# One group of half-row products per half of the heads, in four PSUM banks, in place of two groups in two

## The chip, the cores and the metric

The kernel runs on one core of a Trainium2 chip. The metric is the device time of one execution in microseconds (us). The kernel before takes 2233.55 us, the median of three runs (2233.27 to 2233.9).

An engine is named here as in the profile: PE is TensorE (matmuls; PEld are its weight loads), DVE is VectorE, ACT is ScalarE, POOL is GpSimd, SP is SyncE, whose queue issues most of the DMAs.

## The reference

One decoder layer on 256 tokens of width 2048, in float32: a SwiGLU feed-forward block, a token mixer, a cross-attention into 256 memory rows, a second feed-forward block and a last RMSNorm. The change lies in the mixer's RWKV-7 branch, 16 heads of 64:

```
r, k, v, xw, xa, xg = split(token_shift(p, mu))
w_log = -softplus(-(w0 + tanh(xw) @ w2)) - 0.5          # decay
a     = sigmoid(a0 + xa @ a2)                           # rate
kk    = k * k_k / norm(k * k_k)
k     = k * (1 + (a - 1) * k_a)
y     = scan over t:  S = S * decay_t + (S @ -kk_t) (kk_t * a_t)^T + v_t k_t^T ;  y_t = S @ r_t
```

Here `xw` and `xa` have 64 columns each, so the products with `w2` and `a2` contract over 64 rows. The scan is worked out in two chunks of 128 tokens. In a chunk each head has a triangular system, whose 128x128 matrix holds the products of the removal keys of any two tokens, cut to its lower triangle. These products too contract over 64 rows, the size of a head.

## The kernel before

**The stream of weights.** All large products take 128 tokens by 512 columns and run over the weights in pieces of two times 128 rows. Each float32 weight is divided into a high part (a cast on ACT, line 365) and a low part (a subtraction on DVE, line 366), and each product is three matmuls (lines 442 to 444). SP's queue loads the weights in the order of a plan (line 316). Two pieces ahead of the one in use are divided already.

**The side work.** All else in the mixer is written as generators in groups (`feat`, `attn`, `ew`, `chain`, `norm` and others). In `product`, after each six matmuls of the weight stream, `bg.tick()` lets every group go on by one step, to its next `yield`. `idle(n)` is n steps of nothing. The group `ew` runs one generator at a time, in this order: `decay_and_rate`, `removal_keys` for the first and the second half of the heads, `substitute`, and later `receptances` and `values`. What is traced in this order gives each instruction its priority; the scheduler that draws up the engines' programs takes of the ready ones the one of highest priority. So an instruction whose bank isn't empty can be passed by a later one.

**The banks.** PSUM has eight banks here: three with the tag `acc` (the sums of the weight products), three with the tag `mm` and two with the tag `tr`. `mm()` and `tr()` take the next free bank of their tag. Transposes (`feat`, line 630), the attention's second product (line 996, emptied by lines 1003 and 1004) and the head sums of the keys (line 1158) use `tr`.

**Decay and rate.** `decay_and_rate` waits until attention has been traced, loads `w2` into partitions 0 to 63 and `a2` into 64 to 127 (lines 1059 and 1060), and then goes over the two halves of the heads (`h`) and over two pairs of 128-column pieces in each (`q`). A group is four calls (line 1073): two pieces, and for each the decay (rows 0 to 63, first bank) and the rate (rows 64 to 127, second bank). Four sigmoids on ACT (line 1080) empty the two banks, and two steps of idling follow. Afterwards come the running sums over time on DVE (line 1087).

**Triangular systems.** `removal_keys(h)` makes the keys of eight heads and ends with two groups, one per chunk (`c`): eight calls (line 1195), four pairs of heads, the even ones on rows 0 to 63 into one bank and the odd ones on rows 64 to 127 into another. A step later DVE masks both banks into the tile `lt` (line 1201), POOL issues the DMA of `lt` to the DRAM tile `ld` (line 1206), and a step ends. Before that, POOL multiplies the keys (lines 1185 and 1186). `substitute` then loads the diagonal blocks back through SP's queue (line 1216), solves them row by row on DVE (lines 1223 and 1228) and writes the result to `xd` (line 1230), which the chains of `pairs` (first product at line 1326) use after `values`.

Of the kernel before, what the change touches and what calls it, by code (L numbers as in the profile page):

```python
# [9 lines left out]
AF = mybir.ActivationFunctionType  # L10
# [5 lines left out]
P = 128  # L16
T = 256
# [119 lines left out]
def decoder_layer(ctx: ExitStack, tc: tile.TileContext, a: dict, out: bass.AP):  # L137
    nc = tc.nc
    act, dve, pool, pe = nc.scalar, nc.vector, nc.gpsimd, nc.tensor
# [23 lines left out]
    def mm():  # L163
        return ps.tile([P, 512], F32, tag="mm", name="mm")

    def tr():
        return ps.tile([P, 512], F32, tag="tr", name="tr", bufs=2)

    def wait_for(name):
        while name not in bg.seen:  # L170
            yield

    def idle(n):
        for _ in range(n):
            yield
# [68 lines left out]
    w0, a0, k_k, k_a, r_k, ln_w, ln_b = (cols[:, 80 + i * 8 : 88 + i * 8] for i in range(7))  # L244
# [25 lines left out]
    for entry in weight_plan(a):  # L270
# [10 lines left out]
        for k in range(k0, k0 + nk, 2 * KU):  # L281
            u = len(units)
            units += [(v, k + i, c, 512) for v, c in zip(w, c0) for i in (0, KU)]
            for i in range(2):
                q = (k - k0) // KU + i
# [587 lines left out]
    with tc.tile_pool(name="mx", bufs=1, reuse_waits="tile") as sp:  # L873
# [3 lines left out]
        def t4(name, shape=(P, 4, T), dt=F32):  # L877
            return sp.tile(list(shape), dt, tag="t4", name=name, bufs=N4)
# [165 lines left out]
        def halves(x):  # L1044
            return x[:].rearrange("p c (b t) -> p (c b) t", b=2)

        xwa = sp.tile([P, T], F32, name="xwa")
# [4 lines left out]
        cs, ee, e0, aa, at_, bt, dec = [], [], [], [], [], [], []  # L1052
        keep2 = keep[:].rearrange("p c t -> p (c t)")

        def decay_and_rate():
            yield from wait_for("small")
            yield from wait_for("attn")
            wa = t4("wa", (P, RW))
            pool.dma_start(wa[0:64, :], W["rwkv_w2"])
            pool.dma_start(wa[64:128, :], W["rwkv_a2"])  # L1060
            with tc.issue_after(at["exp"].ins):
                act.activation(xwa[0:64, :], xwa[0:64, :], AF.Tanh)
                act.activation(xg[:], xg[:], AF.Sigmoid)
            yield
            for h in range(2):
                cs.append(t4("cs"))
                aa.append(t4("aa"))
                for q in (0, 2):
                    b = [mm() for _ in range(2)]
                    for i in range(2):  # L1070
                        for e in range(2):
                            r, c = slice(64 * e, 64 * e + 64), (4 * h + q + i) * P
                            pe.matmul(
                                b[e][:, i * T : (i + 1) * T], wa[r, c : c + P], xwa[r, :],
                                start=True, stop=True,
                            )
                    for i in range(2):
                        for e, (dst, bias) in enumerate(((cs[h], w0), (aa[h], a0))):
                            c = 4 * h + q + i
                            sigmoid = act.activation(  # L1080
                                dst[:, q + i, :], b[e][:, i * T : (i + 1) * T], AF.Sigmoid,
                                bias=bias[:, c : c + 1],
                            )
                    yield from idle(2)
            for h in range(2):
                for c in range(4):
                    dve.tensor_tensor_scan(
                        cs[h][:, c, :], keep2, cs[h][:, c, :], 0.0, ALU.mult, ALU.add
                    )
                    if c % 2:  # L1090
                        yield
                c3 = halves(cs[h])
                mid = stat.tile([P, 8], F32, tag="mid", name="mid")
                dve.tensor_copy(mid[:], c3[:, :, 63])
                dve.tensor_tensor(
                    c3, c3, mid[:].unsqueeze(2).to_broadcast([P, 8, P]), ALU.subtract
                )
                dec.append(stat.tile([P, 4], F32, tag="dec", name="dec"))
                dve.tensor_tensor(dec[h][:], cs[h][:, :, 127], mid[:, 1:8:2], ALU.add)
                yield  # L1100
                with tc.issue_after(sigmoid.ins):
                    act.activation(dec[h][:], dec[h][:], AF.Exp, scale=-DECAY)

                ee.append(t4("ee", (P, 8, P)))
                e0.append(stat.tile([P, 8], F32, tag="e0", name="e0"))
                with tc.issue_after(sigmoid.ins):
                    act.activation(e0[h][:], mid[:], AF.Exp, scale=DECAY)
                    act.activation(ee[h][:], c3, AF.Exp, scale=-DECAY)
                yield
                act.activation(cs[h][:], cs[h][:], AF.Exp, scale=DECAY)  # L1110
                yield
            bg.seen.add("decay")

        bg.spawn("ew", decay_and_rate())


# [27 lines left out]
        def removal_keys(h):  # L1144
            yield from wait_for(f"k{h}")
            yield from wait_for("decay")
            ei = cs[h]
            kk, sq = t4("kk"), t4("sq")
            for i in range(4):
                c = 4 * h + i  # L1150
                act.activation(kk[:, i, :], kt[h][:, i, :], AF.Copy, scale=nk_k[:, c : c + 1])
            yield
            act.activation(sq[:], kk[:], AF.Square)
            yield
            for i in (0, 2):
                b = tr()
                sq2 = sq[:, i : i + 2, :].rearrange("p c t -> p (c t)")
                pe.matmul(b[:], bdones[:], sq2, start=True, stop=True)
                act.activation(sq2, b[:], AF.Sqrt)
                yield  # L1160
                dve.tensor_scalar(sq2, sq2, 1e-12, None, ALU.max)
                for k in range(2):
                    dve.reciprocal(sq[:, i + k, :], sq[:, i + k, :])
                    yield from idle(2)
            dve.tensor_tensor(kk[:], kk[:], sq[:], ALU.mult)
            yield
            at_.append(t4("at"))
            for later, before in ((slice(1, P), ee[h][:, :, : P - 1]), (0, e0[h][:])):
                dve.scalar_tensor_tensor(
                    halves(at_[h])[:, :, later], halves(kk)[:, :, later], DOWN, before,  # L1170
                    ALU.mult, ALU.mult,
                )
            yield
            dve.scalar_tensor_tensor(kk[:], kk[:], -1.0, aa[h][:], ALU.mult, ALU.mult)
            yield
            dve.tensor_tensor(kk[:], kk[:], ei[:], ALU.mult)
            bt.append(kk)
            yield
            for i in range(4):
                c = 4 * h + i  # L1180
                dve.tensor_scalar(
                    aa[h][:, i, :], aa[h][:, i, :], k_a[:, c : c + 1], ok_a[:, c : c + 1],
                    ALU.mult, ALU.add,
                )
            pool.tensor_tensor(kt[h][:], kt[h][:], aa[h][:], ALU.mult)
            pool.tensor_tensor(aa[h][:], kt[h][:], ei[:], ALU.mult)

            for c in range(2):
                cs_ = slice(c * P, (c + 1) * P)
                lt = t4("lt", (P, 8, P))  # L1190
                b = [mm() for _ in range(2)]
                for j in range(4):
                    for e in range(2):
                        r = slice(64 * e, 64 * e + 64)
                        pe.matmul(
                            b[e][:, j * P : (j + 1) * P], at_[h][r, j, cs_], bt[h][r, j, cs_],
                            start=True, stop=True,
                        )
                yield
                for e in range(2):  # L1200
                    dve.tensor_tensor(
                        lt[:, 4 * e : 4 * e + 4, :], b[e][:].rearrange("p (j s) -> p j s", j=4),
                        mask_l[:].unsqueeze(1).to_broadcast([P, 4, P]), ALU.mult,
                    )
                o = h * 16 + c * 8
                pool.dma_start(ld[:, o : o + 8, :], lt[:])
                yield
            yield
# [25 lines left out]
        for h in range(2):  # L1234
            kt.append(t4("kt"))
            columns4(kt[h], 8 + 4 * h, f"k{h}")
            bg.spawn("ew", removal_keys(h))
# [321 lines left out]
        for n in range(4):  # L1559
            s = t4("x2", (P, 2, 512))  # L1560
# [62 lines left out]
        for h in (0, 2):  # L1623
            b = tr()
# [17 lines left out]
    with tc.tile_pool(name="f2", bufs=1, reuse_waits="tile") as sp:  # L1642
# [51 lines left out]
        for t in range(2):  # L1694
            m, r = (stat.tile([P, 1], F32, tag=e, name=e) for e in ("ms", "rs"))
# [58 lines left out]
```

## Time and profile before

| what | value |
| --- | --- |
| median of three runs | 2233.55 us |
| profiled execution | 2234.97 us, its span 2233.2 us |
| granted TensorE clock | 0.999 |
| products for decay and rate (line 1073) | 32 instructions, 846.6 to 860.4 us |
| products for the triangular systems (line 1195) | 64 instructions, 905.6 to 944.1 us |
| masks of the systems (line 1201) | 8 instructions, 0.68 us each |
| substitution (lines 1223 to 1230) | 970.5 to 1027.5 us |

The page of the profile gives busy times, the chain of work that ended last and the costliest groups. The timeline view lists instructions in order of time: start, length, engine, line, operation, output and inputs, shapes, count, and in brackets the idle time before them with what ended it. Neighbours of the same kind stand in one row. The length of a matmul is longer than the time from its start to the next one's, since matmuls overlap; so the text goes by starts.

### The profile page before, as it was taken

Reading aid. Unit: us, or ns where it says so; the run is one execution under the profiler, and the core shown is the slowest. Engines: PE = TensorE matmul, PEld = TensorE weight load, DVE = VectorE, ACT = ScalarE, POOL = GpSimd, SP = SyncE. Lnnn points to the kernel's source line nnn. Section 1 sums busy time; section 2 is a strip of 40 time slices with the busy share of each in tenths; the row PEclk is TensorE's granted clock in tenths of the full one; section 3 lists DMA queues with packets and bytes.
Section 4 is the critical chain, followed back from the end, with each engine's and each line's share of the span. In section 5 each row is a group of like instructions: output and inputs, shape, how many; then the busy total and the mean of one; then the engine's idle time right before and its main releaser. Section 6 shows DMA issues by size and latency. Waiting matters only on the chain.

```text
span 2233.2 us, 28140 instructions
## 1 busy us (share of the span) xinstructions
PE 2218.3 (99%) x10520; PEld 1825.6 (82%) x10520; DVE 1828.1 (82%) x2366; ACT 1248.2 (56%) x1626; POOL 116.6 (5%) x181
## 2 busy tenths in 40 slices
PE   9999999999999999999999999999999999999998
PEld 7888888888888877788888888888888888888876
DVE  7999989898989477877657656547999999999997
ACT  7555555555556468544444546556665565655654
POOL 0000000000001001200221030001000000000000
PEclk9999999999999999999999999999999999999999
DMA  8565566556556545677768688658575576556563
GB/s 303 193 211 199 189 208 201 194 189 212 202 189 199 173 134 153 188 236 208 225 202 277 200 262 282 188 160 279 195 251 194 193 245 207 203 208 220 198 240 137
DMA packets 231561, 466.02 MB, mean 209 GB/s; under 512 B 15521, under 2 KB 17921, under 8 KB 231425
## 3 DMA queue, kind: packets, MB, share of 16 engines
q1 hardware_dynamic: 222256, 438.08, 59.3%
q0 software_dynamic: 7648, 23.52, 3.4%
q10 hardware_dynamic: 1520, 2.63, 0.3%
q8 instruction: 82, 1.34, 0.3%
q14 instruction: 55, 0.44, 0.1%
HBM read 440.49 MB, written 23.59 MB: 208 GB/s over the span
## 4 chain that ended last, share of the span: by engine, by line
PE 91%; DVE 4%; DMA 3%; issue 1%; ACT 1%; SPq 0%; POOL 0%; POOLq 0%; ACTq 0%; DVEq 0%
PE acc L442 18%; PE acc L443 18%; PE acc L444 18%; PE mm L442 8%; PE mm L443 8%; PE mm L444 8%; PE tr L443 2%; PE tr L630 2%; PE tr L442 2%; PE tr L444 2%; DVE lo L366 2%; PE mm L1390 1%; DMA raw<-in_ffn_w_up_dram 1%; PE tr L1326 1%; PE mm L949 0%
## 5 line engine op out<-in xcount | busy, mean ns | idle before, releaser
L365 ACT CAST hi<-raw 128x1024 fp32r<-128x1024 f32 (+1 forms) x768 | 754.9, 993 | 685.6 <-PE acc L444 500.9
L366 DVE TENSOR_TENSOR lo<-raw,hi 128x1024 fp32r<-128x1024 f32 (+1 forms) x768 | 882.5, 1152 | 298.7 <-ACT hi L365 296.2
L442 PE MATMUL acc<-hi,xhi 128*128 128x512 f32 (+1 forms) x1134 | 446.9, 395 | 2.3 <-ACT hi L365 0.8
L443 PE MATMUL acc<-lo,xhi 128*128 128x512 f32 (+1 forms) x1134 | 440.5, 389 | 0.8 <-DVE lo L366 0.8
L444 PE MATMUL acc<-hi,xlo 128*128 128x512 f32 (+1 forms) x1134 | 440.2, 388 | 0.0
L442 PEld LDWEIGHTS acc<-hi,xhi 128*128 128x128 f32 x1134 | 212.8, 188 | 49.4 <-issue 3.7
L443 PEld LDWEIGHTS acc<-lo,xhi 128*128 128x128 f32 x1134 | 213.1, 188 | 44.9 <-DVE lo L366 2.1
L444 PEld LDWEIGHTS acc<-hi,xlo 128*128 128x128 f32 x1134 | 213.0, 188 | 44.2 <-issue 1.3
L373 ACT CAST thi<-raw 128x1024 fp32r<-128x1024 f32 x192 | 200.3, 1052 | 75.2 <-DVE raw L396 50.6
L374 DVE TENSOR_TENSOR tlo<-raw,thi 128x1024 fp32r<-128x1024 f32 x192 | 232.1, 1217 | 0.8 <-ACT thi L373 0.2
L442 PE MATMUL mm<-hi,xhi 128*128 128x512 f32 x402 | 156.6, 389 | 0.0
L443 PE MATMUL mm<-lo,xhi 128*128 128x512 f32 x402 | 156.5, 389 | 0.0
L444 PE MATMUL mm<-hi,xlo 128*128 128x512 f32 x402 | 156.4, 389 | 0.0
L444 PE MATMUL acc<-hi,hlo 128*128 128x512 f32 x372 | 145.4, 391 | 0.0
L443 PE MATMUL acc<-lo,hhi 128*128 128x512 f32 x372 | 145.3, 391 | 0.0
L442 PE MATMUL acc<-hi,hhi 128*128 128x512 f32 x372 | 145.0, 390 | 0.0
L442 PEld LDWEIGHTS mm<-hi,xhi 128*128 128x128 f32 x402 | 75.5, 188 | 16.3 <-ACT hi L365 0.5
L443 PEld LDWEIGHTS mm<-lo,xhi 128*128 128x128 f32 x402 | 75.5, 188 | 15.8
L444 PEld LDWEIGHTS mm<-hi,xlo 128*128 128x128 f32 x402 | 75.5, 188 | 15.7
L443 PEld LDWEIGHTS acc<-lo,hhi 128*128 128x128 f32 x372 | 69.8, 188 | 14.4
L444 PEld LDWEIGHTS acc<-hi,hlo 128*128 128x128 f32 x372 | 69.9, 188 | 14.1
L442 PEld LDWEIGHTS acc<-hi,hhi 128*128 128x128 f32 x372 | 69.9, 188 | 14.1
(400 smaller groups left out, 3548.7 us busy)
## 6 DMA issues: line engine op xcount, KB each, us to landing
raw<-in_ffn_w_down_dram SPq DMA_DIRECT2D x88, 1024.0 KB, 5.2
raw<-in_ffn_w_gate_dram SPq DMA_DIRECT2D x84, 1024.0 KB, 5.2
raw<-in_ffn_w_up_dram SPq DMA_DIRECT2D x78, 1024.0 KB, 6.1
raw<-in_w_in_dram SPq DMA_DIRECT2D x136, 512.0 KB, 3.7
raw<-in_w_out_dram SPq DMA_DIRECT2D x32, 512.0 KB, 4.8
raw<-sums SPq DMA_DIRECT2D x20, 512.0 KB, 6.3
raw<-in_w_proj_attn_dram SPq DMA_DIRECT2D x16, 512.0 KB, 4.3
raw<-in_w_proj_rwkv_dram SPq DMA_DIRECT2D x16, 512.0 KB, 6.0
```

The lines of the kernel that those rows point to most:

```text
L365: at["hi"] = act.copy(hi[:, s], raw[:, s])
L366: at["lo"] = dve.tensor_tensor(lo[:, s], raw[:, s], f32(hi[:, s]), ALU.subtract)
L373: act.copy(hi[:], v[:])
L374: dve.tensor_tensor(lo[:], v[:], f32(hi[:]), ALU.subtract)
L442: pe.matmul(o, xh, hi, start=first, stop=False, **how)
L443: pe.matmul(o, xh, lo, start=False, stop=False, **how)
L444: pe.matmul(o, xl, hi, start=False, stop=last, **how)
L630: pe.transpose(b[:, o : o + P], tok[:, t, col : col + P], ident[:])
L1326: pe.matmul(b[e][:, o : o + P], x1[r, j, cs_], x2[r, j, cs_], start=True, stop=True)
L1390: pe.matmul(vb[:, (o + k) * P : (o + k + 1) * P][:, r], lhs(k, e), rhs[:, k, r], start=first and k + e == 0, stop=True, **ek,)
```

## The change

In `decay_and_rate` the two groups of a half become one. Four banks are taken, two `mm` and two `tr`; pieces 0 and 1 go to `mm`, 2 and 3 to `tr`. The eight sigmoids follow, those of the `tr` banks first, and then four steps of idling in place of two times two.

In `removal_keys` the products of both chunks are made in one group, chunk 0 in two `tr` banks and chunk 1 in two `mm` banks. After one step the masks and the DMA of each chunk follow, each chunk with a step behind it. So a half has one step less than before.

```diff
             for h in range(2):
                 cs.append(t4("cs"))
                 aa.append(t4("aa"))
-                for q in (0, 2):
-                    b = [mm() for _ in range(2)]
-                    for i in range(2):
-                        for e in range(2):
-                            r, c = slice(64 * e, 64 * e + 64), (4 * h + q + i) * P
-                            pe.matmul(
-                                b[e][:, i * T : (i + 1) * T], wa[r, c : c + P], xwa[r, :],
-                                start=True, stop=True,
-                            )
-                    for i in range(2):
-                        for e, (dst, bias) in enumerate(((cs[h], w0), (aa[h], a0))):
-                            c = 4 * h + q + i
-                            sigmoid = act.activation(
-                                dst[:, q + i, :], b[e][:, i * T : (i + 1) * T], AF.Sigmoid,
-                                bias=bias[:, c : c + 1],
-                            )
-                    yield from idle(2)
+                b = [[bank() for _ in range(2)] for bank in (mm, tr)]
+                for i in range(4):
+                    for e in range(2):
+                        r, c = slice(64 * e, 64 * e + 64), (4 * h + i) * P
+                        pe.matmul(
+                            b[i // 2][e][:, i % 2 * T : (i % 2 + 1) * T], wa[r, c : c + P],
+                            xwa[r, :], start=True, stop=True,
+                        )
+                for i in (2, 3, 0, 1):
+                    for e, (dst, bias) in enumerate(((cs[h], w0), (aa[h], a0))):
+                        c = 4 * h + i
+                        sigmoid = act.activation(
+                            dst[:, i, :], b[i // 2][e][:, i % 2 * T : (i % 2 + 1) * T], AF.Sigmoid,
+                            bias=bias[:, c : c + 1],
+                        )
+                yield from idle(4)
...
+            b = [[bank() for _ in range(2)] for bank in (tr, mm)]
             for c in range(2):
                 cs_ = slice(c * P, (c + 1) * P)
-                lt = t4("lt", (P, 8, P))
-                b = [mm() for _ in range(2)]
                 for j in range(4):
                     for e in range(2):
                         r = slice(64 * e, 64 * e + 64)
                         pe.matmul(
-                            b[e][:, j * P : (j + 1) * P], at_[h][r, j, cs_], bt[h][r, j, cs_],
+                            b[c][e][:, j * P : (j + 1) * P], at_[h][r, j, cs_], bt[h][r, j, cs_],
                             start=True, stop=True,
                         )
-                yield
+            yield
+            for c in range(2):
+                lt = t4("lt", (P, 8, P))
                 for e in range(2):
                     dve.tensor_tensor(
-                        lt[:, 4 * e : 4 * e + 4, :], b[e][:].rearrange("p (j s) -> p j s", j=4),
+                        lt[:, 4 * e : 4 * e + 4, :], b[c][e][:].rearrange("p (j s) -> p j s", j=4),
                         mask_l[:].unsqueeze(1).to_broadcast([P, 4, P]), ALU.mult,
                     )
```

## The prediction

> **What bounds the kernel now.** I read the page first, then the granted clock in its slices (full speed all along), then TensorE's own timeline at the two places that the change touches, and only then the queues around them.
>
> ```profile
> span 2233.2 us, 28140 instructions
> PE 2218.3 (99%) x10520; PEld 1825.6 (82%) x10520; DVE 1828.1 (82%) x2366; ACT 1248.2 (56%) x1626; POOL 116.6 (5%) x181
> ...
> PE 91%; DVE 4%; DMA 3%; issue 1%; ACT 1%; SPq 0%; POOL 0%; POOLq 0%; ACTq 0%; DVEq 0%
> ```
>
> TensorE is busy for 2218.3 of 2233.2 us and carries 91% of the chain that ended last. So the time falls only where TensorE gets less to do, or where it stops waiting. All else is worth something only through TensorE.
>
> The weight products run at an even beat, which is the ruler for everything below. The windows view of TensorE in a stretch without small products:
>
> ```profile
> 972.00:1012.00 40.00, 40.00 (x179) 1.00 0.68 201
> ```
>
> 179 matmuls touch the 40 us, two of them begun before it; 40/177 = 0.226. I use 0.227 us from start to start. What a small group costs is the time from the start of the last product matmul before it to the start of the second one after it (by then the beat is back), less one beat for each product matmul in between.
>
> **Decay and rate now** (line 1073, TensorE's timeline; columns: start, length, engine, line, operation, count):
>
> ```profile
> 846.32 0.40 PE L443 MATMUL acc<-lo,xhi 128*128 128x512 f32 x1
> 846.65 0.70 PE L1073 MATMUL mm<-xwa,wa 64*128 64x256 f32 x2
> 847.28 1.52 PE L996 MATMUL tr<-pt,vt 128*64 128x256 f32 x12
> 848.72 1.13 PE L1073 MATMUL mm<-xwa,wa 64*128 64x256 f32 x6
> 849.78 0.50 PE L444 MATMUL acc<-hi,xlo 128*128 128x512 f32 x1
> 850.11 0.39 PE L442 MATMUL acc<-hi,xhi 128*128 128x512 f32 x1
> ...
> 851.27 0.40 PE L444 MATMUL acc<-hi,xlo 128*128 128x512 f32 x1
> 851.59 1.14 PE L1073 MATMUL mm<-xwa,wa 64*128 64x256 f32 x8
> 852.66 0.50 PE L442 MATMUL acc<-hi,xhi 128*128 128x512 f32 x1
> 853.00 0.39 PE L443 MATMUL acc<-lo,xhi 128*128 128x512 f32 x1
> ```
>
> One product call is two instructions in the trace, so a group of four calls is x8: four pairs, each pair running on the two halves of the array's rows at once. The second group costs 853.00 - 851.27 - 2 x 0.227 = 1.28 us. Of that, entering is late by 851.59 - 851.27 - 0.227 = 0.09 and leaving by 853.00 - 852.66 - 0.227 = 0.11. The same query from the middle of this group on shows what a pair inside costs:
>
> ```profile
> 852.13 0.60 PE L1073 MATMUL mm<-xwa,wa 64*128 64x256 f32 x4
> ```
>
> The last two pairs take 0.53 up to 852.66, the first two 0.54. The attention row (x12, six pairs of the same 256 columns) takes 848.72 - 847.28 = 1.44 against 1.07 for four pairs: 0.19 for each further pair. I take 0.21, between 0.19 and 0.27. The first group is not whole: one call goes ahead, attention comes between, three calls follow. It costs 850.11 - 846.32 - 0.45 - 1.44 = 1.90, that is 0.62 more than a whole one.
>
> **Triangular systems now** (line 1195), first half of the heads, then the second:
>
> ```profile
> 905.25 0.39 PE L443 MATMUL acc<-lo,yahi 128*128 128x512 f32 x1
> 905.57 1.16 PE L1195 MATMUL mm<-kk,at 64*128 64x128 f32 x16
> 906.66 0.51 PE L444 MATMUL acc<-hi,yalo 128*128 128x512 f32 x1
> 907.10 1.16 PE L1195 MATMUL mm<-kk,at 64*128 64x128 f32 x8
> 908.18 0.51 PE L442 MATMUL acc<-hi,yahi 128*128 128x512 f32 x1
> 908.62 1.16 PE L1195 MATMUL mm<-kk,at 64*128 64x128 f32 x8
> 909.71 0.51 PE L443 MATMUL acc<-lo,yahi 128*128 128x512 f32 x1
> 910.05 0.40 PE L444 MATMUL acc<-hi,yalo 128*128 128x512 f32 x1
> ```
>
> ```profile
> 940.04 0.39 PE L442 MATMUL acc<-hi,yahi 128*128 128x512 f32 x1
> 940.36 1.16 PE L1195 MATMUL mm<-kk,at 64*128 64x128 f32 x16
> ...
> 941.79 0.63 PE L444 MATMUL acc<-hi,yalo 128*128 128x512 f32 x2
> ...
> 942.72 0.40 PE L444 MATMUL acc<-hi,yalo 128*128 128x512 f32 x1
> 943.04 1.29 PE L1195 MATMUL mm<-kk,at 64*128 64x128 f32 x16
> 944.26 0.50 PE L442 MATMUL acc<-hi,yahi 128*128 128x512 f32 x1
> 944.60 0.40 PE L443 MATMUL acc<-lo,yahi 128*128 128x512 f32 x1
> ```
>
> Here is the find of this reading. In the first half of the heads, the second group is torn: eight instructions for one bank, a weight product, eight for the other bank. Eight alone take as long (908.18 - 907.10 = 1.08) as sixteen in pairs (906.66 - 905.57 = 1.09). The `mm` ring has three banks, two were still full, so only one bank of the second group was to be had at once. Cost of the first half: 910.05 - 905.25 - 4 x 0.227 = 3.89. Second half: 941.79 - 940.04 - 0.45 = 1.30, and 944.60 - 942.72 - 0.45 = 1.43; together 2.73.
>
> **The change, part by part.** The number of products, evictions (16 sigmoids, 8 masked multiplies on VectorE) and DMAs stays. What changes is how often TensorE turns from weight products to half-row products and back, and which banks are waited for.
>
> Triangular systems: 32 instructions in one row, four banks (`tr`, `mm`), no other user of `tr` nearby. Price: a whole group of 16 (1.30) plus eight more pairs. From
>
> ```profile
> 906.12 0.61 PE L1195 MATMUL mm<-kk,at 64*128 64x128 f32 x8
> ```
>
> the first four pairs take 0.55 with an entry of 0.09 in it, so 0.11 to 0.14 each; I take 0.11: 1.30 + 8 x 0.11 = 2.18. If the middle cost as much as a whole group, it would be 1.30 + 1.09 = 2.39. Saved: first half 3.89 - 2.18 = 1.71 (at least 1.50), second half 2.73 - 2.18 = 0.55 (at least 0.34).
>
> Decay and rate, second half of the heads: two groups at 1.28 become one at 1.28 + 4 x 0.21 = 2.12. Saved 0.44, between 0.20 (entry and exit alone) and 0.52 (0.19 a pair). If one `mm` bank is still full when the group comes up, its two calls per bank run apart as in the torn group above: that lost half costs 908.18 - 906.66 - 0.227 = 1.29 where half of a pair group costs 0.65, so the end on the other side is a loss of about 0.6. I take 0.4, the nearer row being the contiguous x8.
>
> Decay and rate, first half: the `tr` banks have just been filled by attention (line 996), and VectorE empties them last:
>
> ```profile
> 850.93 0.74 DVE L1004 TENSOR_TENSOR yalo<-tr,yahi 128x256 fp32r<-128x256 f32 x2
> 851.59 1.66 DVE L1032 SCALAR_TENSOR_TENSOR kt<-d,cols,p 128x256 f32<-128x256 f32 x4
> ```
>
> They are free at 851.67, while TensorE is through with the `mm` half at 849.78. So the `tr` half can't follow at once; it would go where the second group goes now (851.59). I take 0, between a gain of 0.4 (joined) plus 0.62 (first call no longer apart), and a loss of 851.67 - 849.78 = 1.9 if it is queued right behind and TensorE waits.
>
> The steps: decay keeps its eight steps of idling. The keys lose one step per half, so what follows is issued two steps (12 product matmuls, 2.7 us) earlier against the weight products. That moves two DMAs on POOL's queue (line 1206), four on SP's queue (line 1216, which wait for them), and the row-by-row substitution on VectorE. On POOL the two DMAs stay behind the multiplies of lines 1185 and 1186, as now. The end of the substitution is in no hurry:
>
> ```profile
> 1027.53 0.58 POOL L1230 DMA_DIRECT2D xd<-xt x1 [9.55 <-DVE xt L1228]
> L1326 PE MATMUL tr<-at,aa x64: 272/272/373, 1103.7 to 1229.8; 64*128 64x128 f32 x64
> ```
>
> Its result leaves at 1027.5 and the blocks that need it start at 1103.7, held by later products. Taken at 0; the danger on SP's queue is a rival below.
>
> Sum: 1.71 + 0.55 + 0.44 + 0 = 2.7. The profiled execution (2234.97 us, its span 2233.2) would become 2232.3; it stands 1.4 above the median of the runs, 2233.55, from which I take the same 2.7: **2230.9**.
>
> **Rivals.**
>
> *More than the turns.* The first decay group joins and isn't torn (0.4 + 0.62), and TensorE's one long wait of this stage goes with the earlier substitution:
>
> ```profile
> 1015.39 0.39 PE L444 MATMUL acc<-hi,xlo 128*128 128x512 f32 x1
> 1016.42 0.50 PE L442 MATMUL acc<-hi,xhi 128*128 128x512 f32 x1 [0.64 <-DVE ga L1248]
> ```
>
> This gap is 0.80 over the beat, caused by VectorE being behind with the substitution. 2.7 + 1.02 + 0.8 = 4.5: 2229.0. For it: the stage would end up to 2.7 us earlier. Against: line 1004's banks.
>
> *The banks aren't empty in time* (the other side). Were the `tr` half queued right behind the `mm` half, it would stand until line 1004 is done. From 2.7 us of waiting on, this decides. With line 1032 (1.66) ahead of line 1004 on VectorE, the banks come free at 853.33, a wait of 3.55: 2233.55 - 2.7 + 3.55 = 2234.4. The second half meets the same with ScalarE's eight sigmoids
>
> ```profile
> L1080 ACT ACTIVATE cs<-mm,cols x8: 467/472/475, 849.5 to 861.2; 128x256 f32<-128x256 f32 x8
> ```
>
> (3.8 us if one by one) now ahead of it in place of four. The Trainium skill has this as a rule (TensorEngine Tiling (Array Packing), PSUM Bottleneck): packing makes TensorE faster but not the emptying of PSUM, which may become the limit. By that rule it would be 2234.4 and not 2230.9; the torn group at 907.10 agrees that a full bank costs TensorE time, and in that group it is the change that provides the empty ones.
>
> *Weights late.* SP's queue stands behind line 1216 until the systems have landed:
>
> ```profile
> 954.45 2.99 SPq L1216 DMA_DIRECT2D dl<-ld x4
> ACT hi L365 <- DMA raw<-in_w_in_dram: 4.4, 2, 4.1
> ```
>
> ScalarE already waits 4.1 us for the weights behind it, and TensorE just bears that. If one more load, a beat of 12 matmuls (2.7 us) earlier, falls behind it, up to 2.7 us come through: no gain, 2233.6; with two such loads 2236.3.
>
> *Nothing joins.* The order is worked out from readiness, and the torn group shows that calls are parted when their banks differ. If the groups fall apart again: 2233.5.
>
> **How the numbers follow.** Forecast 0.41; more than the turns 0.24; banks not empty 0.14; weights late 0.11; nothing joins 0.10. Within 0.2% (4.5 us, about what a measurement of this kernel can tell from no change) lie the forecast, nothing joins and half of the two slower rivals: 0.63. Faster by more: the second case, whose sum sits on that bound, 0.23 with what the others add. Slower by more: 0.14, where waits for banks and weights come several times. The forecast's own range is 2229.9 to 2231.9. To leave out no more than 2 in 10, I go down to 2228.3 (the first rival and the torn pieces' lower ends) and up to 2235.8 (past the bank wait, to one or two late loads).
>
> **What will show it.** Right: in the profile after, line 1195 in two rows of x32, each 2.0 long and 2.2 in cost; line 1073 in the second half as one x16. The first half of decay still in two pieces around 851. The 0.80 gap before the gate multiply of line 1248, still there or gone, decides on the first rival. Wrong: rows of x8 on line 1195, a TensorE wait named after line 1004, 1080 or 1201, or product matmuls after 955 that wait for line 366.

## The result and the profile after

The changed kernel takes 2240.44 us, the median of eight runs (2239.01 to 2242.41), beside 2234.32 us for the kernel before in the same runs. The ratio is 1.0028, with an interval of 1.0019 to 1.0036: slower by about 6 us, where 2.7 us less was forecast. The profiled execution took 2241.63 us with a span of 2239.8, so the two traces below stand 6.6 us apart (2239.8 against 2233.2).

The page of the profile after: span, busy times, and the chain that ended last.

```profile
span 2239.8 us, 28145 instructions
...
PE 2219.4 (99%) x10520; PEld 1826.8 (82%) x10520; DVE 1828.7 (82%) x2366; ACT 1248.3 (56%) x1626; POOL 117.7 (5%) x181
...
PE 93%; DVE 3%; DMA 1%; issue 1%; ACT 1%; SPq 0%; POOLq 0%; POOL 0%; DVEq 0%; ACTq 0%
```

TensorE's busy time rose by only 1.1 us (2218.3 to 2219.4) while the span rose by 6.6. So most of the loss is waiting, and the page can't say where. To find the place I set the start of each product matmul of after against the start of the same one (the same count from the beginning) before. The difference says how late after is at that point:

| start before, us | after minus before, us | what lies between |
| --- | --- | --- |
| 850.11 | +0.04 | all up to the first decay group |
| 864.89 | +0.90 | decay and rate |
| 913.70 | -0.54 | systems, first half of the heads |
| 955.10 | -1.57 | systems, second half |
| 1085.91 | -1.61 | substitution |
| 1299.99 | +7.07 | the chains of `pairs` |
| end of the span | +6.66 | the rest of the kernel |

Up to 1086 us the change gains 1.6 us. Then 8.7 us are lost within the chains, more than 130 us behind the last instruction of the lines that the diff touches (a DMA at 947.4 us), and they are never won back.

**Decay and rate.** TensorE's timeline after:

```profile
850.16 0.40 PE L442 MATMUL acc<-hi,xhi 128*128 128x512 f32 x1
851.43 1.46 PE L1072 MATMUL tr<-xwa,wa 64*128 64x256 f32 x8 [0.87 <-DVE yalo L1004]
852.82 0.50 PE L443 MATMUL acc<-lo,xhi 128*128 128x512 f32 x1
853.15 0.40 PE L444 MATMUL acc<-hi,xlo 128*128 128x512 f32 x1
...
856.57 0.39 PE L444 MATMUL acc<-hi,xlo 128*128 128x512 f32 x1
856.89 1.14 PE L1072 MATMUL mm<-xwa,wa 64*128 64x256 f32 x8
857.86 1.03 PE L1072 MATMUL tr<-xwa,wa 64*128 64x256 f32 x8
858.82 0.50 PE L442 MATMUL acc<-hi,xhi 128*128 128x512 f32 x1
859.16 0.40 PE L443 MATMUL acc<-lo,xhi 128*128 128x512 f32 x1
```

In the first half the `tr` calls come two products behind the `mm` calls, and TensorE stands for 0.87 us until line 1004 has emptied the first bank. It waits again within the row for the second bank: the row takes 852.82 - 851.43 = 1.39 us where the same eight take 858.82 - 857.86 = 0.96 in the second half. The piece costs 853.15 - 850.16 - 0.45 = 2.54 us where it cost 1.28: 1.26 lost. In the second half the group is whole: 859.16 - 856.57 - 0.45 = 2.14 in place of 2 x 1.28, 0.42 gained. Together 0.84 lost, which is the +0.90 - 0.04 of the table.

**Triangular systems.** First half of the heads, then the second:

```profile
906.16 0.39 PE L443 MATMUL acc<-lo,yahi 128*128 128x512 f32 x1
906.48 1.16 PE L1193 MATMUL tr<-kk,at 64*128 64x128 f32 x16
907.47 1.06 PE L1193 MATMUL mm<-kk,at 64*128 64x128 f32 x16
908.46 0.50 PE L444 MATMUL acc<-hi,yalo 128*128 128x512 f32 x1
908.80 0.39 PE L442 MATMUL acc<-hi,yahi 128*128 128x512 f32 x1
...
936.98 0.61 PE L444 MATMUL acc<-hi,yalo 128*128 128x512 f32 x2
937.61 1.16 PE L1193 MATMUL tr<-kk,at 64*128 64x128 f32 x16
938.61 1.06 PE L1193 MATMUL mm<-kk,at 64*128 64x128 f32 x16
939.60 0.50 PE L442 MATMUL acc<-hi,yahi 128*128 128x512 f32 x1
939.93 0.39 PE L443 MATMUL acc<-lo,yahi 128*128 128x512 f32 x1
```

All 32 instructions of a half follow each other. The first half costs 908.80 - 906.16 - 0.45 = 2.19 (3.89 before), the second 939.93 - 937.20 - 0.45 = 2.28 (2.73 before). The torn group with its eight unpaired calls is gone.

**The chains.** The windows view of TensorE from 1080 to 1290 us (columns: window, length, busy, matmuls, granted clock, DMA share, GB/s), before:

```profile
1080.00:1290.00 210.00, 209.59 (x1384) 1.00 0.73 229
```

and after:

```profile
1080.00:1290.00 210.00, 204.57 (x1346) 0.99 0.69 221
```

TensorE idles for 5.4 us after and for 0.4 before. What it waits for, in the waits view of the same window (total, times, longest), before:

```profile
PE tr L1429 <- DVE mk L1332: 0.3, 1, 0.3
```

and after:

```profile
PE tr L630 <- ACT tok L892: 3.0, 1, 3.0
PE acc L443 <- DVE lo L366: 1.6, 1, 1.6
PE tr L1429 <- DVE mk L1332: 0.3, 1, 0.3
PE tr L1363 <- DVE mk L1332: 0.3, 1, 0.3
```

Two new waits. For the first, ScalarE's timeline after:

```profile
1124.18 1.27 ACT L892 ACTIVATE tok<-acc,rs 128x512 f32<-128x512 f32 x2 [4.68 <-DMA sums<-sg]
```

and the storing of the staged inputs on SP's queue (lines 346 and 358 belong to `stage`, which loads two weight pieces for a later layer part into tiles `su` and `sg`, lets VectorE take their differences, lines 350 to 355, and stores these as `sums`):

```profile
1112.97 0.34 SPq L358 DMA_DIRECT2D sums<-su  x1
1113.37 0.43 SPq L346 DMA_DIRECT2D su<-in_ffn_w_up_dram  x1
1113.89 0.74 SPq L346 DMA_DIRECT2D sg<-in_ffn_w_gate_dram  x1
1117.11 0.37 SPq L316 DMA_DIRECT2D raw<-in_w_in_dram  x1
1117.53 0.46 SPq L358 DMA_DIRECT2D sums<-sg  x1
```

`tok` takes its buffer from the same ring (`t4`) as `su` and `sg`, and it got one whose store was not done: that store left 4.6 us behind its twin, behind two new loads and a weight, and landed at 1124.1. The tile itself was done by 1113.7:

```profile
1112.98 0.69 DVE L355 TENSOR_TENSOR sg<-sg,su 128x512 f32<-128x512 f32 x1
```

The queue stood from 1114.6 to 1117.1 because the weight in front of the store waited for its own buffer (the waits view of the queue names line 366). Before, the two stores leave 0.7 us apart:

```profile
1112.06 0.34 SPq L358 DMA_DIRECT2D sums<-su  x1
1112.79 0.34 SPq L358 DMA_DIRECT2D sums<-sg  x1
```

The second wait, on VectorE's timeline after:

```profile
1180.00 0.42 DVE L1484 TENSOR_TENSOR gl<-g,gh 128x256 fp32r<-128x256 f32 x1
1183.52 0.69 DVE L350 TENSOR_TENSOR sg<-su,sg 128x512 f32<-128x512 f32 x1 [3.10 <-issue]
1184.12 0.69 DVE L636 TENSOR_TENSOR yrlo<-yq,yrhi 128x512 fp32r<-128x512 f32 x1
1184.73 0.69 DVE L351 TENSOR_TENSOR su<-su 128x512 f32<-128x512 f32 x1
1185.33 1.22 DVE L366 TENSOR_TENSOR lo<-raw,hi 128x1024 fp32r<-128x1024 f32 x1
```

VectorE stands 3.1 us in front of a staging subtraction, and the low part of the next weight (line 366), queued behind it, comes late. Its high part, which it needs, was done on ScalarE by 1180.6:

```profile
1179.54 1.04 ACT L365 CAST hi<-raw 128x1024 fp32r<-128x1024 f32 x1 [1.65 <-PE acc L444]
```

The Trainium skill (Perfetto Trace Analysis, Tensor Engine Instruction) says that VectorE takes its instructions strictly in order; the trace agrees, since line 366 starts only after the three that stood ahead. The view of line 346 names its own loads as what the first of these, line 350, waited for, 3.1 us once. This load of `sg` was issued at 1172.29 and landed 11.1 us later; before, the longest landing of these loads is 10.5 us.

A third piece of the loss is TensorE's clock. The windows view of TensorE after, with the columns as above:

```profile
1120.00:1130.00 10.00, 6.97 (x36) 0.83 0.21 80
1126.00:1128.00 2.00, 2.00 (x9) 0.50 0.00 0
```

Behind the first wait the granted clock is one half, and two products that follow each other start 0.44 us apart, about twice the beat:

```profile
1125.12 0.65 PE L442 MATMUL acc<-hi,xhi 128*128 128x512 f32 x1
1125.56 0.63 PE L443 MATMUL acc<-lo,xhi 128*128 128x512 f32 x1
```

A mean of 0.83 over 10 us comes to 3.4 us at half the clock, or 1.7 us lost (an estimate from this row). Before, the mean over the whole stage is 1.00.

### The profile page after: what moved, and what is told of

Same layout as the page of the kernel before. It is cut to its first block, busy times and chain, and to the rows that moved or that the text cites. A ratio compares the mean times of both kernels' runs of the same rounds, so it can differ in the third digit from the quotient of the medians.

```text
span 2239.8 us, 28145 instructions
## 1 busy us (share of the span) xinstructions
PE 2219.4 (99%) x10520; PEld 1826.8 (82%) x10520; DVE 1828.7 (82%) x2366; ACT 1248.3 (56%) x1626; POOL 117.7 (5%) x181
## 4 chain that ended last, share of the span: by engine, by line
PE 93%; DVE 3%; DMA 1%; issue 1%; ACT 1%; SPq 0%; POOLq 0%; POOL 0%; DVEq 0%; ACTq 0%
PE acc L442 19%; PE acc L443 19%; PE acc L444 18%; PE mm L443 8%; PE mm L444 8%; PE mm L442 8%; PE tr L630 2%; PE tr L443 2%; PE tr L442 2%; PE tr L444 2%; DVE lo L366 1%; PE mm L1390 1%; PE tr L1326 0%; ACT hi L365 0%; PE mm L949 0%
```

## The experiments

Why should joining products at 906 us disturb a buffer at 1124? *Theory A*: the lost steps. `removal_keys` has one `yield` less per half, so all that the group `ew` issues later comes two steps (12 product matmuls) earlier in program order, also where it isn't ready yet, and the scheduler then orders chains, staging and buffers differently. *Theory B*: the joined groups themselves, in the `tr` banks. The table has every run; the chain stage is the stretch of the same 450 product matmuls from 1080.94 us (before) on, the turns are the times that TensorE goes from products to side work in it, and the span is given against before.

| kernel | median us | ratio, interval | span, us | chain stage, us | turns |
| --- | --- | --- | --- | --- | --- |
| before | 2234.24 to 2234.41 | | 2233.2 | 197.97 | 52 |
| the change | 2240.44 | 1.0028, 1.0019 to 1.0036 | +6.66 | 206.65 | 56 |
| systems, same steps | 2233.06 | 0.9994, 0.9985 to 1.0003 | -2.15 | 197.98 | 52 |
| whole change, same steps | 2233.99 | 0.9999, 0.9990 to 1.0008 | -1.23 | 197.98 | 52 |
| two steps fewer, nothing else | 2242.12 | 1.0035, 1.0023 to 1.0047 | +7.15 | 205.75 | 56 |
| decay alone | 2235.38 | 1.0005, 0.9996 to 1.0013 | +0.16 | 197.97 | 52 |
| systems, steps given back late | 2232.15 | 0.9989, 0.9981 to 0.9998 | -3.18 | 197.98 | 52 |
| combined version | 2231.62 | 0.9987, 0.9978 to 0.9996 | -3.91 | 197.99 | 52 |
| change, staging later | 2237.55 | 1.0015, 1.0006 to 1.0024 | +2.38 | 202.97 | 56 |
| before, staging later | 2234.59 | 1.0000, 0.9991 to 1.0009 | -0.08 | 197.82 | 52 |
| change, staging apart | 2233.57 | 0.9998, 0.9988 to 1.0007 | -2.08 | 198.93 | 54 |
| combined, one step earlier | 2234.84 | 1.0003, 0.9993 to 1.0012 | +0.45 | 200.98 | 51 |
| combined, one step later | 2234.33 | 0.9999, 0.9989 to 1.0008 | -0.86 | 200.19 | 50 |

Single spans carry up to 0.6 us that arises ahead of the change (the difference at 850 us runs from -0.37 to +0.58) and up to 1.1 us that arises behind the chains (from 1300 us to the end of the span), so stages are compared within a trace.

**The steps against the banks.** Four kernels. First the systems alone as in the change, with the lost step given back at the end of each half:

```diff
                 o = h * 16 + c * 8
                 pool.dma_start(ld[:, o : o + 8, :], lt[:])
                 yield
             yield
+            yield
```

> Only the triangular systems are joined, and one empty step is put back at the end of each half, so that all later work keeps the place against the weight products that it has before. Theory A (steps): the loss of the change lies in the stage of the chains, 1086 to 1279 us, because what follows is issued two steps earlier there; with the steps put back that stage is as before and only the gain of the joined groups is left, 1.44 + 1.05 = 2.5 us as read from the two traces: ratio 0.9989, time 2.5 us below before. Theory B (banks): groups in four banks are themselves the loss, since later users of these banks are held up: 4 to 6 us above before.

Then the whole change with the same extra `yield`:

> The whole change, with one empty step put back at the end of each half. Theory A (steps): the gain of the systems, 2.5 us, less what decay and rate lost in the trace after, 0.9 us: 1.6 us below before, ratio 0.9993. Theory B (banks): as the change itself, about 6 us above before.

Then the kernel before with one `yield` taken from the end of `removal_keys`, no product moved:

```diff
                 pool.dma_start(ld[:, o : o + 8, :], lt[:])
                 yield
-            yield
```

> The kernel before, all groups as before, with the last empty step of each half of the keys taken out, and nothing else. Theory A (steps): the stage of the chains takes 8.7 us more, as in the change, and nothing is gained ahead of it: 7 to 9 us above before, ratio 1.003 to 1.004. Theory B (banks): within 1 us of before.

And the change of `decay_and_rate` alone:

> Only decay and rate are joined into groups of four banks; the systems and all steps are as before. Theory A (steps): 0.9 us above before, all of it at 850 us, where the second half of the first group waits for the banks that line 1004 empties; the stage of the chains is as before. Theory B (banks): the tr banks taken here hold up later work too, 3 us or more above before. My forecast had 0.4 us below before.

The kernel with nothing but the missing steps shows the loss: +7.8 us in the chain stage, and the same two waits of TensorE, together 0.9 us shorter than in the change.

```profile
PE tr L630 <- ACT tok L892: 2.7, 1, 2.7
PE acc L443 <- DVE lo L366: 1.0, 1, 1.0
```

The half clock is there too (a mean of 0.83 from 1125 to 1135 us).

Both kernels with joined groups and the old number of steps keep the chain stage of before to 0.01 us. Theory B has fallen and Theory A stands. Decay alone came as expected here, not as the prediction had it: 0.91 us are lost between 850 and 865, about what the two pieces of the change came to (1.26 lost, 0.42 gained). The systems with the same steps missed their size, and with them the whole change with the same steps: they save 1.42 us in the first half of the heads but nothing in the second. There a wait for the bank that the gate multiply empties (line 1248 before, 1250 here), 0.19 us before, now falls behind the joined group and takes the gain:

```profile
949.18 0.50 PE L442 MATMUL acc<-hi,xhi 128*128 128x512 f32 x1 [0.79 <-DVE ga L1250]
```

**Steps given back in a better place.** If only the place of what follows counts, the steps can be given back in front of the substitution, and the second half may keep its step of advance:

```diff
         def substitute():
-            yield from idle(4)
+            yield from idle(6)
```

> The systems alone come as one group per half; the step that each half loses stays lost, and the two steps are given back only in front of the substitution. Theory A (steps): the second half's group comes one step earlier, as in the changed kernel, so both halves save (1.43 + 1.05 = 2.5 us), and the chain stage keeps its 198 us: span about 2230.7, ratio about 0.9989. Rival (it is the joined groups in the `tr` banks, or any earlier second half, that upset the chains): the chain stage grows by 6 us or more and the ratio is 1.002 or higher.

The systems save 1.44 us in the first half and 1.04 in the second, and the chain stage is untouched: 2232.15 us, as expected. With the decay groups joined only in the second half of the heads (the first half goes the old way):

```diff
             for h in range(2):
...
+                if h == 0:
+                    for q in (0, 2):
...
+                    continue
+                b = [[bank() for _ in range(2)] for bank in (mm, tr)]
```

> As the kernel with the systems joined and the steps given back before the substitution, and decay and rate joined only for the second half of the heads; the first half's two groups stay apart, as before. Theory A: 2.5 us of the systems plus 0.4 of decay: span about 2230.3, ratio about 0.9987, faster than both kernels. Rival (the wait for line 1004's banks only moves to the second half): the 0.4 doesn't come, ratio 0.9989 or higher.

Theory A's numbers hold. The combined version takes 2231.62 us and its ratio 0.9987 (0.9978 to 0.9996) excludes 1: it is faster than the kernel before and than the change. Against the version without decay (0.9989) the medians can't tell. The gain of decay shows within the trace, -0.39 us between 850 and 865. The waits view from 1080 to 1290 us is as before the change:

```profile
PE tr L1448 <- DVE mk L1351: 0.3, 1, 0.3
```

**What the lost 8.7 us are made of.** The changed kernel, and then the kernel before, with staging asked for later. `STAGE_AT` counts items; an item is one weight piece, which is two steps, so the edit moves staging by two items or four steps, not by the one item of the expectations:

```diff
-STAGE_AT = [266 + 2 * n for n in range(10)]
+STAGE_AT = [268 + 2 * n for n in range(10)]
```

> The changed kernel, with the staging of the later inputs asked for one item (two steps) later; nothing else. Theory A1 (the loss is two waits behind the staging tiles): the two gaps of 3.4 and 2.0 us in the chain stage go, which gives back 5 of the 8.7 us lost there: about 2235, ratio 1.0005. Theory A2 (the loss is in the order of the products and side work, the waits only its sign): other waits take their place, 2238 to 2241, ratio 1.002 to 1.003.

> The kernel before, with the staging of the later inputs asked for one item (two steps) later; TensorE's order stays as it was. Theory A1: what matters is where staging stands to the chains; here it is moved against chains that stay, two steps as in the change but the other way about, and the waits stay out: within 0.1% of before (2233 to 2236). Theory A3 (any two-step move of staging costs waits): 2 to 6 us more.

The wait for `tok` is gone, 3.7 us of the 8.7 come back, and no other wait takes its place; the wait for line 366 stays, and so does the half clock (a mean of 0.83 from 1180 to 1190 us):

```profile
PE acc L443 <- DVE lo L366: 1.7, 1, 1.7
PE tr L1429 <- DVE mk L1332: 0.3, 1, 0.3
PE tr L1363 <- DVE mk L1332: 0.3, 1, 0.3
```

I had expected both to go. Before, the same move does nothing (1.0000). The expectation has its direction wrong: the change brings the chains forward and leaves staging in place, so against the chains staging comes later there too, by two steps. Counted like this, before has 0 steps and a chain stage of 198.0 us, the change 2 and 206.7, before with later staging 4 and 197.8, the change with later staging 6 and 203.0. So it isn't the distance between the two that costs; that it is how the single tiles and loads happen to fall is my reading. One rival fits these four as well: that the chains cost by standing two steps early against the weight products, as they do in both slow ones. The next run bears on it too. To reach the second wait, the change with the later staging also gets VectorE's subtractions, and the stores behind them, two steps further behind their loads:

```diff
             nc.sync.dma_start(e[:], w[rows, c0 : c0 + 512].rearrange("(a p) n -> p a n", p=P))
-        yield from idle(4)
+        yield from idle(6)
```

> The changed kernel with the staging of the later inputs asked for two steps later and, besides, VectorE's first two subtractions of a staged input put two steps further behind its loads. Theory A1 (what is left of the loss in the chain stage is VectorE standing for a staging load that lands late): the gap of 2.06 us at line 443 goes too, so 1.5 to 2 us less than with the later staging alone: span about 2233.7, ratio 1.0005 to 1.0008. Theory A2 (it is the order that costs): another wait takes its place, ratio 1.0015 as there or higher.

This gave back 4.0 us of the median, where 1.5 to 2 was expected. Now TensorE's waits in the window come to 0.8 us and line 892 finds its buffer free:

```profile
PE tr L1363 <- DVE mk L1332: 0.5, 2, 0.3
PE tr L1429 <- DVE mk L1332: 0.3, 1, 0.3
```

```profile
1115.67 1.27 ACT L892 ACTIVATE tok<-acc,rs 128x512 f32<-128x512 f32 x2
```

The chain stage takes 198.93 us: 7.7 of the 8.7 us are back, although the chains still start two steps early, and the granted clock is 1.00 from 1080 to 1290 us. So the rival falls, and nearly the whole loss hangs on how staging and chains meet. The two gaps themselves (1121.51 to 1124.93 and 1184.65 to 1186.60 on TensorE's timeline after) make up 5.37 us less two beats, 4.9. About 1.7 more is the half clock behind the first. The remaining 2 us went with them; whether as four more turns of TensorE or in another way isn't shown, since the moved staging also changes the order of TensorE's work in this stage (54 turns).

**One step to either side.** The combined version with the substitution one step earlier and one later, `idle(5)` and `idle(7)`:

> The combined version (systems joined, decay and rate joined for the second half), with the substitution one step earlier than there, so that the chains start one step early against the products in place of none. Theory A as a rule of distance (each step early costs half of the 8.7 us): chain stage about 202, ratio about 1.0007. Theory A as a matter of order (the planner's order either falls into the bad one or doesn't): 198 or 206, ratio 0.9987 or 1.0025.

> The combined version with the substitution one step later than there, so that the chains start one step late against the products. If the place of before were a best one, found by tuning, a step to this side costs too: chain stage 200 or more, ratio 0.9995 to 1.002. If only early is harmful: chain stage 198, ratio 0.9987.

Earlier costs 3.0 us in the chain stage, 2.0 of them between two product starts (1175.74 to 1177.75), with VectorE's line 366 named again. Here VectorE waits for no load: it works without a break from 1168.9 to 1179.5, with staging subtractions ahead of line 366. The granted clock stays at 1.00 behind this gap. Later costs 2.2, with no single long wait (0.8 us in two) but more time for the small products (91.11 us in all, 89.37 in the combined version). For the step early, the rule of distance (about 202) came nearer to the 201.0 than all or nothing; for the step late, the expectation that this side costs too held. The place of before is the best of the four tried, and the cost isn't in proportion to the distance (3.0 us for one step early, 8.7 for two).

## Why the prediction failed, step by step

- **The steps: this is the one that failed.** The prediction said of the end of the substitution that it "is in no hurry: ... Its result leaves at 1027.5 and the blocks that need it start at 1103.7, held by later products. Taken at 0". The observation was right (the result left at 1024.7 in after, and the view of `xd` names nobody who waited for it), and the conclusion wrong. What moved by two steps was not only the substitution but everything behind it in the group `ew`: the chains' first product came from 1103.7 to 1099.4 us while the products there ran only 1.6 early. These 2.7 us rearranged the chains against the staging: 8.7 us, of which 4.9 are two waits and about 1.7 the half clock behind the first; about 2 stay unassigned. The same two steps given back in front of the substitution leave the chain stage as it was (197.98). No run separates the substitution itself from what follows it in the group. I had counted the instructions of the moved step and its DMAs, but not the program order of all that is traced after it.
- **Systems:** forecast 1.71 and 0.55, by the same rule 1.70 and 0.45. In the table's differences the first half keeps 1.44, since small delays of products behind the group give 0.26 back. The second half comes to 1.03: the wait for the bank that line 1248 empties, 0.35 us over the beat at 950.2 before, shrank to 0.05, and a delay of 0.25 ahead of the group (at 937.5 before) is absent after. In sum 2.5 against 2.26; that this is so near is in part luck, since neither of these two was in the sum.
- **Decay, second half:** forecast 0.44, came to 0.42.
- **Decay, first half:** taken at 0 and cost 1.26. This was the rival *the banks aren't empty in time*, at its place and with its name (line 1004), but at a third of its price of 3.55: VectorE did line 1004 ahead of line 1032, so the banks came free at 851.4 and 851.7 and not at 853.33. The scheduler did not put the calls right behind the `mm` half, as that rival feared; it put them two products on, 0.87 us too early for the first bank.
- **More than the turns:** false on both counts; the first decay group didn't join, and the long wait before line 1248 stayed (0.62 us at 1014.84 where it was 0.64 at 1016.42).
- **Weights late:** didn't come; up to 1086 us no product waits for line 366. One does at 1186.6, a sign of being wrong that the prediction had named, but behind a staging load and not behind line 1216.
- **Nothing joins:** false; two rows of x16 follow each other in both halves.
- **The range** ended at 2235.8, since all its mechanisms lay between 846 and 1030 us. The mechanism that decided lay outside of this window, in a part of the trace that was looked at only for the question whether the substitution is late.

## What to carry to other kernels

Where order is drawn up from the place in the program, a step removed from a group moves everything behind it in that group, ready or not, against all other groups; so look at the stage in which those later parts meet other work, however far away, and price its shared buffers and queues. The remedy is cheap to try: make the local gain and give the lost steps back at the point behind which nothing should move. Joining small half-row products is worth what the turns cost (1.7 us for a torn group, 0.4 for a whole one), but only with banks that are empty by then.

## What was unexpected in the hardware's behaviour

- A kernel with one empty step less per half, whose products are the same, takes 0.35% more (1.0035, 1.0023 to 1.0047). With TensorE busy for 99% of the span, order alone still decides on 8 us.
- A store on a queue that also carries loads can leave late: 4.6 us lie between two stores that leave 0.7 us apart before, 2.5 of them because a weight load ahead on the queue waited for its buffer. It held a buffer on which ScalarE, and then TensorE, stood for 3 us.
- A DMA landing 11.1 us after its issue (10.5 at most before) came through to TensorE by way of an engine that isn't short of time: VectorE was at 82%, but it stood in front of the late one with an urgent instruction behind it.
- Behind waits of TensorE of 3.0 us (the change), 2.7 us (two steps fewer) and 1.7 us (change, staging later; there 2 us behind the wait's end) the granted clock stood at 0.50 for about 3.4 us, some 1.7 us of work lost besides the wait. The length alone doesn't decide: behind one of 1.6 us (combined, one step earlier) it stayed at 1.00, behind one of 1.5 us near the start (combined, one step later, at 10.5 us) it fell. That the waits cause it isn't tested.
